# Spreading the differential heads' norm factors over the partitions: through DRAM instead of through TensorE

## The chip, the core and the metric

The kernel runs on one core of a Trainium2 chip. Such a core has five engines that each work through their own queue in order: TensorE (PE in the profile; its weight loads are PEld), VectorE (DVE), ScalarE (ACT), GpSimd (POOL) and SyncE (SP). SP and POOL issue the DMAs of this kernel; the transfers themselves run on 16 DMA engines. The metric is the device time of one execution in microseconds.

## The reference, cut to what matters

One decoder layer on 512 tokens of width 1024: two attention branches side by side, a gated merge, and a gated MLP. The branch that the change touches is differential attention with four heads. Each head has two softmax maps, takes their weighted difference, multiplies it with values of width 128, and then applies an RMS norm per head and token:

```python
def block_fn(args):
    qblk, n = args
    scores = jnp.einsum('bqhmd,bshmd->bhmqs', qblk, k).astype(jnp.float32) * scale
    ...
    p = jax.nn.softmax(scores, axis=-1)
    a = p[:, :, 0] - lam * p[:, :, 1]
    return jnp.einsum('bhqs,bshe->bqhe', a.astype(v.dtype), v)
...
out = out.reshape(b, s, DIFF_HEADS, DIFF_VDIM)
out = _rmsnorm(out, subln_g) * (1.0 - lam_init)
...
merged = (jax.nn.sigmoid(ga) * (out_a @ w_branch_swa[l])
          + jax.nn.sigmoid(gd) * (out_d @ w_branch_diff[l]))
```

So every head yields 512 norm factors, one for each token, and each of a head's 128 output channels of that token is multiplied by it.

## The kernel before, in words

All matrices are held as pairs of a rounded part (`hi`, made by a cast on ScalarE) and its remainder (`lo`, made by a subtraction on VectorE). A product is three matmuls: hi by hi, hi by lo, lo by hi (`mm3`, lines 121 to 124).

The differential stage lies at about 130 to 240 us of the span. Its outputs are kept transposed, with the 128 channels of a head on the partitions and the 512 tokens along the free dimension. The norm factors come out the other way round: `stats` (line 802) sums the squares with small matmuls into a tile of 128 partitions by 4 columns, token 128 n + p at partition p and column n, and VectorE and GpSimd turn these into the factors `rs` (the tile is `drs` in the profile). The factor has to be multiplied along the free dimension, alike on all partitions. So `turn_norm` (line 812) lets TensorE transpose each of the four columns, broadcast to 128 columns, into a PSUM bank `rb` of 128 by 512, which then holds the factors in every partition. VectorE multiplies the head's output `of` by it (line 816), ScalarE casts the product into `outd` hi, VectorE subtracts for `outd` lo (`split`, lines 117 to 119).

The order of TensorE's work is written out by hand. Beside the attention blocks run the projections of later steps: `fill(n)` (line 540) issues n steps of them, three matmuls of 512 columns each, and counts them. A piece of work can be hung on that count: `after(n, fn)` calls `fn` n steps later, `flush(kind)` calls what was put by under a kind. The loop over the 16 blocks s (head h = s // 4, block n = s % 4) fills 2 and then 4 steps a block, issues scores, softmax and transpositions (`td` in the profile, of the softmax results `sd`), and at n = 0 the values of the head before (`diff_values`). The sums of a head are flushed in the third block of the next head, its norm in the first block of the head after that, 12 steps later. The last head has no such blocks behind it: its sums come 10 steps (STAT_LAG) after its values, its norm 16 steps (NORM_LAG) after that.

The order on VectorE and ScalarE in this stage is not written out; the framework's scheduler chooses it from priorities and its own estimate, with some pieces pinned behind others (`tc.issue_after`). VectorE also prepares the weights (subtractions at line 119), adds up rows of the conditioning matrix (`arow`, lines 857 and 859, from tiles `ra` that SP loads), and evacuates score and transposition banks.

GpSimd's queue has little in this stage: per head one power for the norm (line 185), per finished conditioning row one small write to DRAM (`mod_rows`, line 882), and at its end the loads of `g1b` and its bias, which spread a conditioning row over all partitions (line 1067). The merge of the branches reads all four heads' `outd` from its first step on (`pB` in the profile).

Of the kernel before, what the change touches and what calls it, by code (L numbers as in the profile page):

```python
# [34 lines left out]
ADA_START = 4  # L35
V_LAG = 13
STAT_LAG = 10
NORM_LAG = 16
SWA_FILL = (2, 2, 5, 2, 2, 2, 2, 3)
DIFF_FILL = (3, 2, 4, 2)  # L40
WARM_FIRST = 3
# [13 lines left out]
def kernel(  # L55
# [44 lines left out]
    def tbank(name, shape=(P, S)):  # L100
        return bank("t", 2, list(shape), name)
# [15 lines left out]
    def split(hi, lo, src):  # L117
        cast = nc.scalar.copy(hi, src)
        return cast, nc.vector.tensor_sub(lo, src, hi.bitcast(F32))
# [368 lines left out]
    def evac(hi, lo, src, scale=None):  # L488
        if scale is None:
            nc.scalar.copy(hi, src)  # L490
            nc.vector.tensor_sub(lo, src, hi.bitcast(F32))
        else:
            nc.scalar.activation(hi, src, AF.Copy, scale=scale)
            return nc.vector.scalar_tensor_tensor(lo, src, scale, hi.bitcast(F32), ALU.mult, ALU.subtract)
# [66 lines left out]
            if tick[0] >= ADA_START and tick[0] % ADA_EVERY == 0:  # L561
                next(ada, None)

    beside = {"row": [], "sum": [], "norm": [], "turn": []}

    def after(n, fn):
        later.append([n, fn])
# [13 lines left out]
    hT = (hTh, hTl)  # L581


    class Pair:
        pass

    def swa_scores(i, blocks):
        if 0 in blocks:
            c = pairs[i] = Pair()
            c.mx, c.nm, c.lsum, c.es = (  # L590
                ap.tile([P, 2, NT], F32, tag=t, bufs=2, name=f"{t}{i}") for t in ("mx", "nm", "lsum", "es")
            )
            c.sb = [ap.tile([P, 2, P], F32, tag="st0", bufs=2, name=f"st{i}_0")]
            c.sb += [ap.tile([P, 2, 256], F32, tag="st", bufs=ST, name=f"st{i}_{n}") for n in range(1, NT)]
            c.pT = []
        c = pairs[i]
        sps = {
            (g, j): vbank(f"sw{i}_{g}_{j}").rearrange("p (a q) -> p a q", a=2)
            if len(blocks) == NT and (g, j) == (1, 1) else sbank(f"sw{i}_{g}_{j}", (P, 2, 256))
            for g in sorted({n // 2 for n in blocks}) for j in range(2)  # L600
        }
        for n in blocks:
            w = P if n == 0 else 2 * P
            k0 = max(0, n - 1) * P
            qs, ks = slice(n * P, (n + 1) * P), slice(k0, k0 + w)
            mm3_rows([
                (
                    sps[n // 2, j][:, n % 2, :w],
                    [qa[64 * j : 64 * j + 64, i, b, qs] for b in range(2)],
                    [ka[64 * j : 64 * j + 64, b, ks] for b in range(2)],  # L610
                )
                for j in range(2)
            ])
        for n in blocks:
            w = P if n == 0 else 2 * P
            if n == 2:
                c.first = c.last
            for j in range(2):
                with tc.high_priority(offset=HP):
                    c.last = nc.vector.tensor_tensor_reduce(  # L620
                        c.sb[n][:, j, :w], sps[n // 2, j][:, n % 2, :w], dsw[:, 256 - w : 256], 1.0, -3e38, ALU.add, ALU.max,
                        c.mx[:, j, n : n + 1],
                    )
# [151 lines left out]
    def diff_transpose(s):  # L775
        h, n = divmod(s, NT)
        if n == 0:
            aTs[h] = [ap.tile([P, 1664], F32R, tag=g, bufs=2, name=f"{g}{h}") for g in ("aTh", "aTl")]
        tp = tbank(f"td{h}_{n}")
        for k in range(n + 1):  # L780
            nc.tensor.transpose(tp[:, k * P : (k + 1) * P], probs[s][:, k * P : (k + 1) * P], ident)
        hi, lo = (a.rearrange("p (b q) -> p b q", q=P)[:, n : 4 * n + 1 : 3] for a in aTs[h])
        with tc.high_priority(offset=HP):
            evac(hi, lo, tp[:, : (n + 1) * P].rearrange("p (k q) -> p k q", q=P))

    def diff_values(h):
        t, (aTh, aTl) = heads[h], aTs[h]
        o = vbank(f"od{h}")
        for k in range(NT):
            q0 = k * P  # L790
            mm3(
                o[:, q0:], t[:, 4, k * P : (k + 1) * P], t[:, 5, k * P : (k + 1) * P],
                aTh[:, k * AW + q0 : k * AW + 512], aTl[:, k * AW + q0 : k * AW + 512],
                k == 0, k == NT - 1,
            )
        sq = ap.tile([P, S], F32, tag="tmp", bufs=2, name=f"sq{h}")
        of = ap.tile([P, S], F32, tag="of", bufs=2, name=f"of{h}")
        nc.scalar.activation(sq, o, AF.Square)
        nc.scalar.activation(of, o, AF.Copy, scale=sublnc)

        def stats():
            pss = tbank(f"pss{h}", (P, NT))
            for n in range(NT):
                nc.tensor.matmul(pss[:, n : n + 1], sq[:, n * P : (n + 1) * P], ones[:, 0:1], start=True, stop=True)
            rs, r0, r2 = (ap.tile([P, NT], F32, tag=t, bufs=2, name=f"{t}{h}") for t in ("drs", "dr0", "dr2"))
            nc.vector.reciprocal(r0, sums[h][:, 0])
            nc.vector.tensor_mul(r2, r0, r0)
            nc.vector.tensor_mul(r2, r2, pss)
            rstd_m2(rs, r2, NT, P, ap)
            nc.vector.tensor_mul(rs, rs, r0)  # L810

            def turn_norm():
                rb = tbank(f"rb{h}")
                for n in range(NT):
                    nc.tensor.transpose(rb[:, n * P : (n + 1) * P], rs[:, n : n + 1].to_broadcast([P, P]), ident)
                nc.vector.tensor_mul(of, of, rb)
                split(outd[0][:, h], outd[1][:, h], of)

            if h < 3:
                beside["norm"].append(turn_norm)  # L820
            else:
                after(NORM_LAG, turn_norm)

        if h < 3:
            beside["sum"].append(stats)
        else:
            after(STAT_LAG, stats)


    mod_rows = tc.dram_tile([4, D], F32, name="mod_rows")  # L830

    def ada_load(idx, hf, k):
        c0 = (2 + idx) * D + hf * S
# [55 lines left out]
    def add_gate_a(j):  # L889
        def gate(wts):  # L890
            o = fbank(f"pga{j}")
            yield from steps(o, wts, hT, KT)
            nc.scalar.activation(ta[:, j], o, AF.Tanh, scale=0.5)

        def load():
            if j % 2 == 0:
                r = raw_tile([P, 4, 2 * P], f"wba{j}")
                for a in range(2):
                    nc.sync.dma_start(
                        r[64 * a : 64 * a + 64],  # L900
                        wba[256 * a : 256 * a + 256, j * P : (j + 2) * P].rearrange("(i p) n -> p i n", p=64),
                    )

                with tc.issue_after(spread[-1].ins) if j == 0 else ExitStack():
                    pair_w["a"] = split_pair(r, [P, 4, 2 * P], f"wba{j}")
            return pair_w["a"]

        def branch(wts):
            o = fbank(f"pA{j}")
            rhs = [[outa[b][:, k] for k in range(4)] for b in range(2)]  # L910
            yield from steps(o, wts, rhs, 4, cl=slice(j % 2 * P, j % 2 * P + P))
            nc.vector.scalar_tensor_tensor(ta[:, j], ta[:, j], 1.0, o, ALU.add, ALU.mult)

        units.append((lambda: load_cols(win, COL_GA + j * P, f"wga{j}"), gate))
        units.append((load, branch))

    group_ahead, sums = [1], {}
    pairs, firsts, scored, probs, aTs = {}, {}, {}, {}, {}
    ada = ada_rows()
    add_head(0)  # L920
# [47 lines left out]
    for s in range(4 * DIFF_HEADS):  # L968
        h, n = divmod(s, NT)
        if s in (4, 8):  # L970
            add_head(h + 1)
        elif s == 12:
            add_gate_a(2)
            add_gate_a(3)
        ahead = s == 1
        fill(DIFF_FILL[1] - ahead)
        nxt = (s + 1, s + 2) if n % 2 and s < 15 else ()
        if nxt:
            flush("row")
            diff_scores(*nxt)  # L980
        if n == 1:
            diff_transpose(s)
        fill(DIFF_FILL[2] + ahead)
        if n == 2:
            flush("sum")
        elif n == 0:
            flush("norm")
        if n != 1:
            diff_transpose(s)
        if s == 13:  # L990
            group_ahead.clear()
        elif s > 13:
            flush("row")
        diff_softmax(*nxt)
        if n == 0 and h:
            diff_values(h - 1)
            fill(DIFF_FILL[3])
    for j in range(4, KT):
        add_gate_a(j)
    fill(4)  # L1000
    flush("norm")
    diff_values(DIFF_HEADS - 1)
    while units or loaded or current:
        fill(1)
# [936 lines left out]
```

## Time and profile before

| what | value |
|---|---|
| median of 3 runs | 692.78 us (692.33 to 694.1) |
| the profiled execution | 693.06 us, its span 691.3 us |
| granted TensorE clock | 0.996 |
| TensorE busy | 680.5 us, 98% of the span |
| VectorE busy | 565.3 us, 82% |
| ScalarE busy | 384.6 us, 56% |
| GpSimd busy | 82.1 us, 12% |
| transpositions of norm factors | 16 in 4 blocks, starting at 161.8 to 229.7 us |

In a row of a timeline the first number is the start in us from the span's start, the second the duration; then engine, line, operation, output tile <- input tiles, shapes, and in brackets how long the engine stood idle before and what ended that. In a row of stages stand the busy times of TensorE, its weight loads, VectorE, ScalarE and GpSimd, each with its count, then the granted clock, the DMA engines' busy share and GB/s. The matmuls' durations overlap: one starts before the one before it has ended.

### The profile page before, as it was taken

To read this page: it belongs to the slowest core of one execution; us is meant where nothing else is said; L and a number is where in the kernel's file an instruction comes from. 1 tells how busy PE (TensorE), PEld (TensorE's weight loads), DVE (VectorE), ACT (ScalarE), POOL (GpSimd) and SP (SyncE) were. 2 spreads that over 40 slices of the span, in tenths; PEclk is the share of its full clock that TensorE was granted. 3 is DMA by queue.
4 is the path that set the end of the run, shared out by engine and by line. 5 is a ranking of instruction groups with operands and counts; after the bars stand their busy time and mean duration, and the time that the engine had idled before them with its cause. 6 is when DMAs were issued, how large, how long until landed. Compare 5 with 4: busy or idle time off the path is not lost. (4 is left out here: it accounts for less than half of the span.)

```text
span 691.3 us, 11249 instructions
## 1 busy us (share of the span) xinstructions
PE 680.5 (98%) x4203; PEld 592.7 (86%) x4203; DVE 565.3 (82%) x1073; ACT 384.6 (56%) x686; POOL 82.1 (12%) x100
## 2 busy tenths in 40 slices
PE   8999999999999999999999999999999999999995
PEld 5787877788888888888889999999999999888884
DVE  5898987987885666663789988888888999979997
ACT  7676666545552323332477756655565666656665
POOL 3000000000001000000030101112111002540300
PEclk9999999999999999999999999999999999999998
DMA  9985454553455675229726798777978748997903
GB/s 307 328 258 165 140 156 151 154 163 96 138 138 169 212 217 180 91 95 315 230 56 129 166 214 197 167 173 215 206 215 217 155 149 207 196 195 199 167 1 121
DMA packets 115926, 121.81 MB, mean 176 GB/s; under 512 B 4447, under 2 KB 93344, under 8 KB 115872
## 3 DMA queue, kind: packets, MB, share of 16 engines
q1 hardware_dynamic: 96958, 95.09, 43.8%
q0 software_dynamic: 18720, 25.73, 22.2%
q8 instruction: 33, 0.54, 0.3%
q10 hardware_dynamic: 194, 0.28, 0.1%
q14 instruction: 21, 0.17, 0.1%
HBM read 118.97 MB, written 2.11 MB: 175 GB/s over the span
## 5 line engine op out<-in xcount | busy, mean ns | idle before, releaser
L1270 PE MATMUL up<-t,m_whi 128*128 128x256 f32 x512 | 93.1, 283 | 0.0
L1270 PEld LDWEIGHTS up<-t,m_whi 128*128 128x128 f32 x512 | 79.9, 192 | 0.0
L1270 PE MATMUL up<-t,m_wlo 128*128 128x256 f32 x256 | 72.4, 283 | 0.0
L1270 PE MATMUL up<-bh,p_whi 128*128 128x256 f32 x232 | 65.7, 283 | 0.0
L1270 PE MATMUL up<-bl,p_whi 128*128 128x256 f32 x232 | 65.7, 283 | 0.0
L1270 PE MATMUL up<-bh,p_wlo 128*128 128x256 f32 x232 | 65.7, 283 | 0.0
L859 DVE SCALAR_TENSOR_TENSOR arow<-ra,cs,arow 128x512 f32<-128x512 f32 x56 | 42.0, 749 | 20.0 <-DMA ra<-in_w_ada_dram 19.4
L1270 PEld LDWEIGHTS up<-t,m_wlo 128*128 128x128 f32 x256 | 49.2, 192 | 0.0
L1270 PEld LDWEIGHTS up<-bh,p_whi 128*128 128x128 f32 x232 | 44.5, 192 | 0.0
L1270 PEld LDWEIGHTS up<-bl,p_whi 128*128 128x128 f32 x232 | 44.5, 192 | 0.0
L1270 PEld LDWEIGHTS up<-bh,p_wlo 128*128 128x128 f32 x232 | 44.5, 192 | 0.0
L1179 POOL DMA_DIRECT2D s<-in_w_up_dram x21 | 27.0, 1361 | 140.8 <-DMA s<-in_w_up_dram 66.5
L1207 ACT CAST m_whi<-s 128x1024 fp32r<-128x1024 f32 x31 | 32.5, 1049 | 11.1 <-DVE s L1201 6.3
L1211 DVE TENSOR_TENSOR m_wlo<-s,m_whi 128x1024 fp32r<-128x1024 f32 x31 | 37.8, 1219 | 0.0
L1270 PE MATMUL up<-t,p_whi 128*128 128x256 f32 x176 | 32.2, 283 | 0.0
L882 POOL DMA_DIRECT2D mod_rows<-row x8 | 4.9, 614 | 204.9 <-ACT row L881 204.9
L1270 PEld LDWEIGHTS up<-t,p_whi 128*128 128x128 f32 x176 | 27.5, 192 | 0.0
L1277 ACT ACTIVATE gT<-a,cv 128x512 f32<-128x512 f32 x22 | 17.8, 816 | 16.9 <-DVE a L1312 15.8
L185 POOL TENSOR_TENSOR r<-ms,mhalf 128x1 f32<-128x1 f32 (+1 forms) x16 | 12.6, 791 | 120.9 <-DVE ms L183 73.1
L1207 ACT CAST p_whi<-wa 128x1024 fp32r<-128x1024 f32 x18 | 18.8, 1046 | 12.5 <-PE up L1270 12.5
L1211 DVE TENSOR_TENSOR p_wlo<-wa,p_whi 128x1024 fp32r<-128x1024 f32 x18 | 22.0, 1223 | 3.8 <-ACT p_whi L1207 3.8
L1270 PE MATMUL up<-t,p_wlo 128*128 128x256 f32 x88 | 24.9, 283 | 0.0
(491 smaller groups left out, 2064.9 us busy)
## 6 DMA issues: line engine op xcount, KB each, us to landing
ra<-in_w_ada_dram SPq DMA_DIRECT2D x32, 512.0 KB, 4.4
wa<-in_w_up_dram SPq DMA_DIRECT2D x22, 512.0 KB, 3.9
s<-in_w_up_dram SPq DMA_DIRECT2D x21, 512.0 KB, 4.5
s<-in_w_up_dram POOLq DMA_DIRECT2D x21, 512.0 KB, 6.6
adaw<-in_w_ada_dram SPq DMA_DIRECT2D x12, 512.0 KB, 7.6
w<-in_w_in_dram SPq DMA_DIRECT2D x12, 512.0 KB, 4.9
a<-in_w_up_dram SPq DMA_DIRECT2D x11, 512.0 KB, 4.5
b<-in_w_down_dram SPq DMA_DIRECT2D x10, 512.0 KB, 4.6
```

The lines of the kernel that those rows point to most:

```text
L185: nc.gpsimd.tensor_tensor(r0, ms, mhalf[:, :n], ALU.pow)
L859: nc.vector.scalar_tensor_tensor(ac, r[:, a], cc, ac, ALU.mult, ALU.add)
L882: nc.gpsimd.dma_start(mod_rows[idx, hf * S : (hf + 1) * S].rearrange("(g n) -> g n", g=4), row[0:P:32])
L1179: nc.gpsimd.dma_start(dst, upblock(*blk), accum_op=ALU.add)
L1207: nc.scalar.copy(W[J, name][0], R[J, SRC[name]])
L1211: nc.vector.tensor_sub(lo, R[J, SRC[name]], hi.bitcast(F32))
L1270: nc.tensor.matmul(o[u], w[:, k, cu], b[:, k], start=name in ("p1", "m5", "p2") and k == 0 and x == 0, stop=k == 3 and x == 2, skip_group_ ...
L1277: nc.scalar.activation(grow(j), av[J][:, u], AF.Identity, bias=cv[:, 66 + j : 67 + j], scale=cv[:, 44 + j : 45 + j])
```

## The change

The factors of a head go from SBUF to a row of 512 numbers in DRAM (`norm_rows`), with 4 bytes per run because they lie across the partitions, and from there a second DMA reads the row into all 128 partitions of `rb`, now an SBUF tile. Both are issued on GpSimd's queue, at the end of `stats`. The second waits for the first. `rb` takes the place of the tiles that held the first blocks of the sliding-window attention: these two are now one explicit tile `st0` with two halves, and `rb` has one buffer under the same tag. The product and its split (`scale_out`) are hung 24 steps behind the sums for all four heads, and pinned on VectorE behind the last evacuation recorded before them (`read`). The flush of the norms goes away; before the last head's values stand 6 steps instead of 4 and a flush. In the order of the changed program TensorE has four entries fewer (16 transpositions in blocks of four), GpSimd's queue eight DMAs more, and SP's queue is the same.

```diff
-NORM_LAG = 16
+NORM_LAG = 24
...
-            nc.vector.tensor_sub(lo, src, hi.bitcast(F32))
+            return nc.vector.tensor_sub(lo, src, hi.bitcast(F32))
...
+    st0 = ap.tile([P, 2, 2, P], F32, tag="st0", name="st0")
...
-            c.sb = [ap.tile([P, 2, P], F32, tag="st0", bufs=2, name=f"st{i}_0")]
+            c.sb = [st0[:, i % 2]]
...
-            evac(hi, lo, tp[:, : (n + 1) * P].rearrange("p (k q) -> p k q", q=P))
+            read.append(evac(hi, lo, tp[:, : (n + 1) * P].rearrange("p (k q) -> p k q", q=P)))
...
-            def turn_norm():
-                rb = tbank(f"rb{h}")
-                for n in range(NT):
-                    nc.tensor.transpose(rb[:, n * P : (n + 1) * P], rs[:, n : n + 1].to_broadcast([P, P]), ident)
-                nc.vector.tensor_mul(of, of, rb)
-                split(outd[0][:, h], outd[1][:, h], of)
-
-            if h < 3:
-                beside["norm"].append(turn_norm)
-            else:
-                after(NORM_LAG, turn_norm)
+            rb = ap.tile([P, S], F32, tag="st0", name=f"rb{h}")
+            nc.gpsimd.dma_start(norm_rows[h].rearrange("(n p) -> p n", p=P), rs)
+            nc.gpsimd.dma_start(rb, norm_rows[h].partition_broadcast(P))
+
+            def scale_out():
+                with tc.issue_after(read[-1].ins):
+                    nc.vector.tensor_mul(of, of, rb)
+                    split(outd[0][:, h], outd[1][:, h], of)
+
+            after(NORM_LAG, scale_out)
...
+    norm_rows = tc.dram_tile([DIFF_HEADS, S], F32, name="norm_rows")
...
-            nc.vector.scalar_tensor_tensor(ta[:, j], ta[:, j], 1.0, o, ALU.add, ALU.mult)
+            read.append(nc.vector.scalar_tensor_tensor(ta[:, j], ta[:, j], 1.0, o, ALU.add, ALU.mult))
...
-        elif n == 0:
-            flush("norm")
...
-    fill(4)
-    flush("norm")
+    fill(6)
     diff_values(DIFF_HEADS - 1)
```

More of the change, by code (lines that the diff above doesn't have):

```diff
@@ L562, in fill @@
                 next(ada, None)
-    beside = {"row": [], "sum": [], "norm": [], "turn": []}
+    beside = {"row": [], "sum": [], "turn": []}
     def after(n, fn):
@@ L911, in branch @@
             yield from steps(o, wts, rhs, 4, cl=slice(j % 2 * P, j % 2 * P + P))
-            nc.vector.scalar_tensor_tensor(ta[:, j], ta[:, j], 1.0, o, ALU.add, ALU.mult)
+            read.append(nc.vector.scalar_tensor_tensor(ta[:, j], ta[:, j], 1.0, o, ALU.add, ALU.mult))
         units.append((lambda: load_cols(win, COL_GA + j * P, f"wga{j}"), gate))
         units.append((load, branch))
-    group_ahead, sums = [1], {}
+    group_ahead, sums, read = [1], {}, []
     pairs, firsts, scored, probs, aTs = {}, {}, {}, {}, {}
```

## The prediction

> **What bounds the kernel now.** I read the page's first part, then who waited for whom on TensorE, then the busy times by stage, and only then single tiles. The first fence is the page's share of busy time, the longest of TensorE's waits inside the attention stages, and the busy time by stage.
>
> ```profile
> span 691.3 us, 11249 instructions
> PE 680.5 (98%) x4203; PEld 592.7 (86%) x4203; DVE 565.3 (82%) x1073; ACT 384.6 (56%) x686; POOL 82.1 (12%) x100
> ...
> PE tp L656 <- DVE st L644: 0.5, 1, 0.5
> ...
> 130.00:240.00 110.00, 110.00 (x612) 89.34 (x611) 83.12 (x209) 50.46 (x109) 8.79 (x13) 1.00 0.53 157
> 240.00:580.00 340.00, 339.88 (x2396) 318.72 (x2395) 275.81 (x390) 181.58 (x271) 36.95 (x35) 1.00 0.68 179
> 580.00:684.00 104.00, 103.87 (x473) 86.32 (x471) 97.44 (x147) 63.98 (x97) 28.58 (x26) 1.00 0.74 149
> ```
>
> From 130 us to 684 us TensorE (first busy column) is never without a matmul for more than 0.25 us in all, at full granted clock (the 1.00). So every microsecond of TensorE issue taken out of the differential stage (130 to 240) should move all that follows, and every wait put in front of TensorE should push it back. VectorE has 83 of 110 us busy there, so it has room, but it works in order: a wait on it can reach TensorE.
>
> **Part 1, the transpositions go.** Rows of the transposed factors, and the matmuls around two of the four blocks (start, duration):
>
> ```profile
> L815 PE MATMUL rb<-ident,drs x16: 271/272/273, 161.8 to 229.8; 128*128 128x128 f32 x16
> L816 DVE TENSOR_TENSOR of<-of,rb x4: 687/689/689, 162.5 to 230.1; 128x512 f32<-128x512 f32 x4
> L119 DVE TENSOR_TENSOR outdB<-of,outdA x4: 685/690/693, 163.8 to 233.0; 128x512 fp32r<-128x512 f32 x4
> ...
> 161.82 0.60 PE L815 MATMUL rb<-ident,drs 128*128 128x128 f32 x4
> 162.26 0.27 PE L781 MATMUL td<-ident,sd 128*128 128x128 f32 x1
> ...
> 229.23 0.39 PE L124 MATMUL pga<-hThA,wga_l 128*128 128x512 f32 x1
> 229.46 0.60 PE L815 MATMUL rb<-ident,drs 128*128 128x128 f32 x4
> 229.81 0.48 PE L122 MATMUL pga<-hThB,wga_h 128*128 128x512 f32 x1
> 230.13 0.39 PE L123 MATMUL pga<-hTlB,wga_h 128*128 128x512 f32 x1
> ```
>
> A transposition lasts 272 ns, but matmuls overlap, so starts count. A matmul of 512 columns is followed after 0.23 us (229.23, 229.46). Around the last block, 229.23 to 230.13 is 0.90 us for two such matmuls, which by themselves take 0.45: the block costs 0.45. The first block holds its follower back from 161.82 to 162.26: 0.44. Taken for four heads: 4 x 0.445 = 1.8 us. Bounds: 0.35 per block (229.46 to 229.81), 1.4 us; and all sixteen durations, 16 x 0.272 = 4.4 us. I take 1.8, since starts are what TensorE's queue passes on. The Trainium skill, "TensorE: Matmul & The Clock Gate", Part 4: PE-mode transpose, puts a transposition inside a kernel at about 275 ns; by that the gain would be 16 x 0.275 = 4.4 us. The row's 272 ns agrees with it, the spacing of starts does not.
>
> VectorE's product reads the factors from SBUF instead of PSUM. Its row is 689 ns, and the subtraction beside it, all from SBUF, 690: zero.
>
> **Part 2, two DMAs per head on POOL's queue.** No row shows a DMA of 4-byte runs. Nearest rows: POOL's issue of 512 runs (L1179), the small write to DRAM (landing least, median, most), and POOL's broadcast reads.
>
> ```profile
> L1179 POOL DMA_DIRECT2D s<-in_w_up_dram x21 | 27.0, 1361 | 140.8 <-DMA s<-in_w_up_dram 66.5
> ...
> DMA to landing us min/median/max: 1.6/3.1/4.2
> ...
> s_t<-in_w_up_dram POOLq DMA_DIRECT2D x1, 512.0 KB, 11.3
> g1b<-mod_rows POOLq DMA_DIRECT2D x1, 512.0 KB, 4.8
> xn<-in_b_ada_dram POOLq DMA_DIRECT2D x1, 512.0 KB, 5.7
> g2b<-mod_rows POOLq DMA_DIRECT2D x2, 256.0 KB, 6.2
> ```
>
> The write also has 512 runs (128 partitions x 4): 1.4 us to issue, 3.1 to land. The read is g2b's twin, 256 KB out of a 2 KB row: 6.2. Chain: 10.7 us. Bounds: 1.6 + 4.8 = 6.4, and 1.4 + 4.2 + 11.3 = 16.9. I take 10.7, by the twin.
>
> How long may it be? VectorE meets the wait where the changed program has the product. That order shows it behind the reciprocal that ran at 174.09 (head 0), and behind the `ta` products at 196.85, 218.80 and 236.53 (heads 1 to 3). The rows: factors ready (drs), that predecessor, the next softmax product (sd), and TensorE's transposition (td) that needs it.
>
> ```profile
> 156.47 0.16 DVE L810 TENSOR_TENSOR drs<-drs,dr 128x4 f32<-128x4 f32 x1
> 174.09 0.16 DVE L767 RECIPROCAL dls<-dls 128x1 f32<-128x1 f32 x1
> 175.91 0.61 DVE L769 SCALAR_TENSOR_TENSOR sd<-sd,dls,sd 128x384 f32<-128x384 f32 x1
> 177.24 0.53 PE L781 MATMUL td<-ident,sd 128*128 128x128 f32 x3
> 181.60 0.16 DVE L810 TENSOR_TENSOR drs<-drs,dr 128x4 f32<-128x4 f32 x1
> 194.50 0.68 DVE L744 CUSTOM_DVE_ANT_0 sd<-sd,ddf 128x512 f32<-128x512 f32 x1
> 196.19 0.74 DVE L859 SCALAR_TENSOR_TENSOR arow<-ra,cs,arow 128x512 f32<-128x512 f32 x1
> 196.85 0.68 DVE L912 SCALAR_TENSOR_TENSOR ta<-ta,pA 128x512 f32<-128x512 f32 x1
> 196.96 0.37 SPq L835 DMA_DIRECT2D ra<-in_w_ada_dram  x1
> 198.10 0.62 DVE L769 SCALAR_TENSOR_TENSOR sd<-sd,dls,sd 128x384 f32<-128x384 f32 x1
> 200.77 1.54 DVE L859 SCALAR_TENSOR_TENSOR arow<-ra,cs,arow 128x512 f32<-128x512 f32 x2 [0.50 <-DMA ra<-in_w_ada_dram]
> 201.49 0.53 PE L781 MATMUL td<-ident,sd 128*128 128x128 f32 x3
> 205.84 0.16 DVE L810 TENSOR_TENSOR drs<-drs,dr 128x4 f32<-128x4 f32 x1
> 216.19 0.62 POOL L882 DMA_DIRECT2D mod_rows<-row  x1 [12.48 <-ACT row L881]
> 218.80 0.68 DVE L912 SCALAR_TENSOR_TENSOR ta<-ta,pA 128x512 f32<-128x512 f32 x1
> 221.85 0.16 DVE L810 TENSOR_TENSOR drs<-drs,dr 128x4 f32<-128x4 f32 x1
> 236.53 0.68 DVE L912 SCALAR_TENSOR_TENSOR ta<-ta,pA 128x512 f32<-128x512 f32 x1
> 237.13 1.22 DVE L1075 TENSOR_TENSOR g1b<-g1b,xn 128x1024 f32<-128x1024 f32 x1
> 253.63 0.39 PE L122 MATMUL pB<-outdA,wbd 128*128 128x512 f32 x1
> ```
>
> Windows from factors ready to predecessor's end: 174.25 - 156.63 = 17.6; 197.53 - 181.76 = 15.8; 219.48 - 206.0 = 13.5; 237.2 - 222.0 = 15.2 us. All exceed 10.7, so I cost the chain at nothing; its cover is 24 steps of projection matmuls. If that cover fails, the price is rival C.
>
> Queued behind the two on POOL: the next `mod_rows` write (closest behind head 2: 216.19, 10.2 us after its factors, while the chain holds POOL for 4.5 and 0.6) and then the next head's power; nothing lost. After head 3 the loads of `g1b` and its bias stand behind the read, which waits for the write: 222.0 + 4.5 for the write, 0.6 for each of two issues, then 5.7 to land the bias: near 233.4. VectorE adds them at 237.13: hidden by 3.7 us. SP's queue keeps its order.
>
> One buffer now serves all four `rb`, so head h's read waits for head h-1's product. The program puts each product before the next head's factors: nothing.
>
> **Part 3, the product moves later.** From 12 steps after the sums (head 2: 10, head 3: 16) to 24; head 3's values come two steps later, because two steps replace the last flush. TensorE does the same steps, in another order: zero. The consumer is the merge at 253.63; head 3's product near 237.9, its cast and subtraction (0.69) end by 240: 13 us to spare.
>
> On VectorE the product now stands in denser work. Head 0: sd's 384-wide product ended at 176.52 and TensorE wanted it at 177.24; the changed order has one `arow` step fewer ahead of it and the product (0.69 for 0.75), while TensorE comes 0.44 earlier: about 0.3 us spare. Head 1: product and one `arow` step stand ahead of sd, and that step waits for `ra`, which landed at 200.77, 3.8 after its issue at 196.96, itself released by the `arow` step at 196.19. In the changed order the releasing step stands ahead of the score reduction at 194.50: done near 194.9, landing near 198.7, then `arow` (0.75) and sd (0.62) by 200.0, TensorE there at 201.49 - 0.9 = 200.6: 0.6 us spare. So zero, but thin.
>
> **The sum.** Transpositions -1.8, all else 0. The profiled execution is 693.06 us (span 691.3, 1.8 around it): 691.3. The median of the runs, 692.78, is 0.3 lower: 691.0.
>
> **The rivals.** **B, a thin spare gives way.** If head 1's `ra` lands 1 to 2 us later, or head 0's sd slips, TensorE waits 0.2 to 1.4 us and the gain is part gone: 691.2 to 692.8, say 692.0. For it: VectorE waited for `ra` at 200.77 already. Against: that load's issue moves forward too.
>
> **C, slower: the DMA chain outgrows its window.** VectorE stops in front of the softmax products, TensorE in front of td. A chain of c us costs c - 17.6 - 0.3 at head 0 and c - 15.8 - 0.6 at head 1 (heads 2 and 3 have no transposition close behind). Gain gone at c = 18.1, slower by 0.3% from c = 19.1, 20 us gives 2.1 + 3.6: 696.7. For it: no row shows 4-byte runs. Against: the upper bound, 16.9, costs only 0.5. The Trainium skill, "SBUF — State Buffer", SBUF: two separate sides, warns that a DMA issued from GpSimd starves while VectorE runs an operation in a two-port mode, and gives 3.1 us for one that takes 0.62 alone. By an estimate from that page two DMAs would add 5 us: a chain of 15.7 and still about 691. No row here shows such a pair.
>
> **D, faster: the whole durations go.** If a block holds TensorE for 4 x 0.272, the gain is 4.4: 688.4. For it the row; against it the starts.
>
> **How the numbers follow.** A (forecast, 690.5 to 691.6) 0.56; B 0.15; C 0.17; D 0.12. A measurement tells 0.3%, 2.1 us, from no change: the bounds are 690.7 and 694.9. A's 1.8 us lies just inside; four tenths of A falls beyond 690.7 with the scatter of the runs (692.33 to 694.1). Faster 0.22 + 0.12 = 0.34; same 0.34 + 0.15 = 0.49; slower 0.17. Range 689.6 to 694.8 leaves out half of D and three quarters of C, 0.19.
>
> **What would show it.** Right: no TensorE gap over 0.3 us between 150 and 240, td of head 1 about 0.9 us earlier, the merge at about 251.9; VectorE's waits for `rb` near zero. Wrong: VectorE waiting for `rb`'s DMA or for `ra` directly before a td, or DMAs of `norm_rows` landing after more than 9 us.

## The result: slower by 4.6%

The changed kernel takes 724.5 us (median of 4 runs, 721.29 to 728.66) against 692.56 us before: a ratio of 1.0463, 95% interval 1.0399 to 1.0527, or some 32 us. The forecast was 691.0 us with a range up to 694.8. The profiled execution of the changed kernel is 728.66 us with a span of 726.8, the longest of its four; against the profiled execution before (span 691.3) it is 35.5 us longer, and the traces below explain that difference.

First the page of the changed kernel: busy times, and the row of VectorE's `arow` steps (busy time, mean ns; idle time before them and what ended it).

```profile
span 726.8 us, 11228 instructions
PE 689.2 (95%) x4187; PEld 598.3 (82%) x4187; DVE 564.3 (78%) x1073; ACT 382.9 (53%) x686; POOL 87.4 (12%) x108
L861 DVE SCALAR_TENSOR_TENSOR arow<-ra,cs,arow 128x512 f32<-128x512 f32 x56 | 41.9, 748 | 58.5 <-DMA ra<-in_w_ada_dram 57.9
```

TensorE's longest waits (total, times, longest, us):

```profile
PE pA L122 <- DVE ta L914: 14.6, 2, 8.3
PE td L783 <- DVE dls L769: 5.1, 1, 5.1
PE td L783 <- DVE sd L771: 2.9, 1, 2.9
PE pss L806 <- DVE qkv L491: 2.0, 1, 2.0
```

VectorE's longest wait, and the same wait in the kernel before:

```profile
DVE arow L861 <- DMA ra<-in_w_ada_dram: 57.9, 14, 14.9
...
DVE arow L859 <- DMA ra<-in_w_ada_dram: 19.4, 15, 2.9
```

The busy time by stage, in the columns of the kernel before:

```profile
130.00:240.00 110.00, 97.18 (x516) 78.32 (x514) 66.28 (x183) 43.33 (x100) 9.59 (x13) 0.92 0.50 113
240.00:580.00 340.00, 326.56 (x2187) 300.41 (x2188) 259.14 (x368) 164.84 (x247) 40.32 (x41) 0.97 0.70 179
```

TensorE, which was busy in all 110 us of the first stretch before, now stands still for 12.8 of them, and the granted clock there is 0.92 instead of 1.00. VectorE did not get more work (564.3 us, 565.3 before): it waited 57.9 us for `ra`, where the kernel before waited 19.4. The stage and its way to the merge are where the difference lies. From the first sums of a head (`pss`) to the first matmul of the gates behind the stage (`pgd`) the kernel before takes 90.6 us (152.2 to 242.8) and the changed one 124.0 (151.9 to 275.9). From there to the merge (`pB`) it is 10.8 and 13.0. What lies before and behind differs by 0.3 us at most.

Of these 35.6 us, TensorE's waits between the first sums and the merge make up 26.3. The rest goes to a lower clock: the trace's clock record shows half the full clock for four stretches of 6.8 to 10.2 us, each during or right behind one of the longer waits, and a matmul of 512 columns then takes 0.63 us in place of 0.39:

```profile
205.51 0.39 PE L124 MATMUL pga<-hThB,wga_l 128*128 128x512 f32 x1
...
216.32 0.63 PE L124 MATMUL pA<-outah,wba_l 128*128 128x512 f32 x1
```

By an estimate from these numbers the lower clock costs some 9 to 11 us: 35.6 less 26.3 is 9.3, and 1.8 more if the transpositions took what the prediction says.

GpSimd's timeline tells what came first: the write of each head, and the read that follows.

```profile
156.65 0.84 POOL L815 DMA_DIRECT2D norm_rows<-drs  x1 [1.08 <-DVE dmx L746]
168.52 0.59 POOL L816 DMA_DIRECT2D rb<-norm_rows  x1 [11.03 <-PE sd L129]
186.26 0.82 POOL L815 DMA_DIRECT2D norm_rows<-drs  x1 [1.10 <-DVE drs L812]
197.04 0.56 POOL L816 DMA_DIRECT2D rb<-norm_rows  x1 [9.95 <-DMA norm_rows<-drs]
220.76 0.82 POOL L815 DMA_DIRECT2D norm_rows<-drs  x1 [2.59 <-DVE drs L812]
233.69 0.56 POOL L816 DMA_DIRECT2D rb<-norm_rows  x1 [12.10 <-DMA norm_rows<-drs]
250.59 0.82 POOL L815 DMA_DIRECT2D norm_rows<-drs  x1 [1.09 <-DVE drs L812]
261.83 0.56 POOL L816 DMA_DIRECT2D rb<-norm_rows  x1 [10.41 <-issue]
```

Rows of the view of DMAs (KB each, median us from issue to landing):

```profile
norm_rows<-drs POOLq DMA_DIRECT2D x4, 2.0 KB, 11.0
rb<-norm_rows POOLq DMA_DIRECT2D x4, 256.0 KB, 5.7
```

The landings of the loads of `ra`, in the changed kernel and in the kernel before:

```profile
DMA to landing us min/median/max: 3.8/4.8/15.4
...
DMA to landing us min/median/max: 3.8/4.4/5.2
```

A write of 2 KB lands after 11.0 us (median), twice as long as the read of 256 KB behind it. And a load of `ra` (512 KB), whose longest landing before was 5.2 us, now takes up to 15.4. VectorE's timeline shows these late loads behind the writes of all four heads, with the long waits at heads 1 to 3:

```profile
171.87 0.49 DVE L859 TENSOR_SCALAR arow<-ra,cs 128x512 f32<-128x512 f32 x1 [4.02 <-DMA ra<-in_w_ada_dram]
201.20 1.54 DVE L861 SCALAR_TENSOR_TENSOR arow<-ra,cs,arow 128x512 f32<-128x512 f32 x2 [8.78 <-DMA ra<-in_w_ada_dram]
237.70 1.54 DVE L861 SCALAR_TENSOR_TENSOR arow<-ra,cs,arow 128x512 f32<-128x512 f32 x2 [14.89 <-DMA ra<-in_w_ada_dram]
244.72 0.68 DVE L914 SCALAR_TENSOR_TENSOR ta<-ta,pA 128x512 f32<-128x512 f32 x1
245.32 0.68 DVE L820 TENSOR_TENSOR of<-of,rb 128x512 f32<-128x512 f32 x1
267.28 1.54 DVE L861 SCALAR_TENSOR_TENSOR arow<-ra,cs,arow 128x512 f32<-128x512 f32 x2 [14.01 <-DMA ra<-in_w_ada_dram]
```

And TensorE's timeline shows what it then waits for:

```profile
214.80 0.87 PE L783 MATMUL td<-ident,sd 128*128 128x128 f32 x3 [5.06 <-DVE dls L769]
245.46 0.80 PE L122 MATMUL pA<-outah,wba_h 128*128 128x512 f32 x1 [8.27 <-DVE ta L914]
270.61 0.79 PE L122 MATMUL pA<-outah,wba_h 128*128 128x512 f32 x1 [6.33 <-DVE ta L914]
```

The last three of the waits shown, 8.78 + 14.89 + 14.01 = 37.7 us, are two thirds of the 57.9; each ends 4.0 to 5.5 us after the read that waits for the write was issued (197.04, 233.69, 261.83). VectorE works in order, so the `ta` products and softmax pieces behind the waiting `arow` step come late, and TensorE stops for them. The product with `rb` (245.32) has no wait of its own in brackets: the row had landed by then. So the loss is not where a reader of the diff would look, in front of `rb`, but in front of another load.

### The profile page after: what moved, and what is told of

Its sections match the earlier page's. It is cut to its first block, busy times and chain, and to the rows that moved or that the text cites. A ratio compares the mean times of both kernels' runs of the same rounds, so it can differ in the third digit from the quotient of the medians.

```text
span 726.8 us, 11228 instructions
## 1 busy us (share of the span) xinstructions
PE 689.2 (95%) x4187; PEld 598.3 (82%) x4187; DVE 564.3 (78%) x1073; ACT 382.9 (53%) x686; POOL 87.4 (12%) x108
## 4 chain that ended last, share of the span: by engine, by line
PE 80%; DMA 12%; DVE 5%; ACT 1%; issue 1%; POOL 0%; SPq 0%; DVEq 0%; ACTq 0%; POOLq 0%
PE up L1269 31%; PE dc L1884 14%; DMA ra<-in_w_ada_dram 10%; PE a L385 3%; PE oc L1325 2%; PE oc L1329 2%; PE oc L1326 2%; PE pgd L122 2%; PE pgd L123 2%; PE pgd L124 2%; DVE arow L861 1%; DMA w<-in_w_in_dram 1%; PE pw L122 1%; PE pB L122 1%; PE pB L123 1%
## 5 line engine op out<-in xcount | busy, mean ns | idle before, releaser
L861 DVE SCALAR_TENSOR_TENSOR arow<-ra,cs,arow 128x512 f32<-128x512 f32 x56 | 41.9, 748 | 58.5 <-DMA ra<-in_w_ada_dram 57.9
L766 ACT ACTIVATE sd<-sd,dmx 128x128 f32<-128x128 f32 (+3 forms) x32 | 17.6, 553 | 26.0 <-DVE dmx L756 26.0
L122 PE MATMUL pA<-outah,wba_h 128*128 128x512 f32 x32 | 15.8, 493 | 14.6 <-DVE ta L914 14.6
```

Source lines behind the costliest of these rows:

```text
L122: nc.tensor.matmul(o, lh, rh, start=start, stop=False)
L766: exp = nc.scalar.activation(pm[m], pm[m], AF.Exp, bias=mx[:, m : m + 1], scale=slope, accum_out=ls)
L861: nc.vector.scalar_tensor_tensor(ac, r[:, a], cc, ac, ALU.mult, ALU.add)
```

## The experiments

A theory to start with: the write of 4-byte runs holds the DMA engines, and all that is loaded meanwhile comes late. Its rivals: the read of 256 KB beside the loads; the new order of VectorE's work; and GpSimd's way of issuing.

**The write alone, the read alone, the order alone, and the write in long runs.**

```diff
 write alone (kernel before, behind the factors)
+            nc.gpsimd.dma_start(norm_rows[h].rearrange("(n p) -> p n", p=P), rs)
 read alone (kernel before; rx in the tile st0)
+            nc.gpsimd.dma_start(rx, final_g[0:S].partition_broadcast(P))
 order alone (changed kernel, no DMAs)
             def scale_out():
+                rb = tbank(f"rb{h}")
+                for n in range(NT):
+                    nc.tensor.transpose(rb[:, n * P : (n + 1) * P], rs[:, n : n + 1].to_broadcast([P, P]), ident)
 rows of 512 bytes (changed kernel, hung 6 steps behind the sums)
 ...
+                nc.tensor.transpose(pn, rs, ident)
 ...
+                    nc.scalar.copy(rows4, pn)
+                nc.gpsimd.dma_start(norm_rows[h].rearrange("(n p) -> n p", p=P), rows4)
+                nc.gpsimd.dma_start(rb, norm_rows[h].partition_broadcast(P))
```

> The kernel before, with only the write added: each head's factors go to DRAM in 512 runs of 4 bytes, nobody reads them, the transpositions stay. Theory W (the write of 4-byte runs holds up the DMA engines, so the weight and conditioning loads come late): 15 to 35 us slower than before, VectorE's waits for ra near 55 us, landing of the write near 11 us. Theory O (the new order on VectorE and the late product): no change, within 2 us. Theory R (the broadcast read): no change, within 2 us.

> The kernel before, with only a broadcast read of 256 KB per head added on GpSimd's queue (a row of an input into all partitions, into the tile that rb has in the changed kernel; nobody uses it), the transpositions stay. Theory W: within 2 us of before. Theory R: 15 to 35 us slower. Theory O: within 2 us.

> The changed kernel without its DMAs: the product 24 steps behind the sums and pinned as there, the last head's values 2 steps later, but the factors spread by TensorE's transpositions just ahead of the product. Theory W: within 2 us of before, no TensorE wait above 1 us in the stage. Theory O: 15 to 35 us slower, VectorE waiting for ra ahead of the softmax products.

> The changed kernel, but one small TensorE transposition turns the 128 by 4 factors into 4 rows of 128, ScalarE copies them to SBUF, and the write goes to DRAM in 4 runs of 512 bytes; read, lag and product as in the changed kernel. Theory W: 690.5 to 693, the write lands in 2 to 4 us, no TensorE wait above 1 us in the stage. Theories O and R: as slow as the changed kernel, 715 to 728.

| kernel | median, us | ratio to before (95%) | write lands, median us | longest `ra`, us |
|---|---|---|---|---|
| write alone | 713.07 | 1.0294 (1.0261 to 1.0328) | 9.9 | 11.4 |
| read alone | 693.19 | 1.0013 (1.0001 to 1.0024) | none | 5.3 |
| order alone | 697.4 | 1.0062 (1.0044 to 1.008) | none | 5.1 |
| rows of 512 bytes | 694.18 | 1.002 (1.0009 to 1.0031) | 2.3 | 5.0 |

The write, which nobody reads and which stands in an otherwise unchanged kernel, costs 20 us. It gives the changed kernel's picture in small, though VectorE waits less for `ra` than the 55 us that were expected. Its longest wait there:

```profile
DVE arow L862 <- DMA ra<-in_w_ada_dram: 40.7, 16, 8.9
```

TensorE's:

```profile
PE td L781 <- DVE dr L806: 5.6, 1, 5.6
PE pA L122 <- DVE ta L915: 5.4, 2, 4.1
```

The landings of its write:

```profile
DMA to landing us min/median/max: 8.9/9.9/10.4
```

The order alone takes 4.3 us more, a figure that none of the theories had. It is not all the order's: of TensorE's 2.9 us of waiting in that stage, 2.1 are this run's own.

```profile
PE td L783 <- DVE of L819: 2.1, 2, 1.9
```

There the transpositions still put `rb` into a PSUM bank of the kind that `td` needs as well, and `td` waits until the product has read it. In the changed kernel `rb` lies in SBUF and this wait cannot come. A cleaner figure stands further down. The same numbers by the same route, but first turned by one TensorE transposition into 4 runs of 512 bytes, cost 1.4 us in place of 32 (expected were 693 us at most). The read alone says less than it was meant to: nothing made it wait, so its four issues ran ahead to 105.3 to 120.0 us, in front of the stage. What a read within the stage costs is told further down.

**What about the write is slow: the number of runs, their size, their distance, or the queue?**

```diff
 a quarter: 128 runs of 4 bytes, 4 bytes apart
+            nc.gpsimd.dma_start(norm_rows[h, 0:P].rearrange("(p n) -> p n", n=1), rs[:, 0:1])
 spread: 512 runs of 4 bytes, 512 bytes apart (16 for P: 64 bytes apart)
+    norm_rows = tc.dram_tile([DIFF_HEADS, NT, P, P], F32, name="norm_rows")
+            nc.gpsimd.dma_start(norm_rows[h, :, :, 0].rearrange("n p -> p n"), rs)
 other queue: as the write alone
+            nc.scalar.dma_start(norm_rows[h].rearrange("(n p) -> p n", p=P), rs)
 runs of 16 bytes (changed kernel)
-            nc.gpsimd.dma_start(norm_rows[h].rearrange("(n p) -> p n", p=P), rs)
+            nc.gpsimd.dma_start(norm_rows[h].rearrange("(p n) -> p n", n=NT), rs)
-                    nc.vector.tensor_mul(of, of, rb)
+                    o3 = of.rearrange("q (n p) -> q n p", p=P)
+                    nc.vector.tensor_mul(o3, o3, rb.rearrange("q (p n) -> q n p", n=NT))
```

> As the write alone, but each head writes only one of its four columns: 128 runs of 4 bytes to DRAM instead of 512; nobody reads them. Write alone with 512 runs cost 20.3 us and landed in 9.9 us. If every run costs time (theory W by runs): landing near 3 to 4 us, 0 to 5 us slower than before. If one such write holds things up whatever its size: landing near 10 us, 15 to 20 us slower.

> As the write alone with all 512 runs of 4 bytes, but every run goes to a DRAM address of its own, 512 bytes from the next, so that no two runs of different DMA engines meet in one piece of memory. If the runs hurt because they are small or many: landing near 10 us and 15 to 20 us slower than before, as the write alone. If they hurt because neighbours in DRAM are written by different engines at once: landing in 2 to 5 us, within 3 us of before.

> As the write alone, 512 runs of 4 bytes to the same DRAM row, but issued on ScalarE's queue instead of GpSimd's. If the DRAM side holds up the DMA engines: landing near 10 us, 15 to 25 us slower than before. If GpSimd's way of issuing does: landing in 2 to 4 us, within 3 us of before (and a wait of ScalarE for the factors).

> The kernel before with a write beside it of 512 runs of 4 bytes that lie 64 bytes apart, read by nobody. With 4 bytes apart the time rose by 20 us, with 512 bytes apart by nothing. If what collides is a stretch of DRAM of some 64 bytes or fewer, it stays at 692 to 694 us with landings of 2 to 4 us. If the stretch is larger (512 runs at 64 bytes take 32 KB, against 256 KB), landings lie between 3 and 9 us and the time rises by some part of the 20 us.

> The changed kernel, but each row of norm factors lies in DRAM as the tile has it: partition p writes its 4 numbers next to each other, 128 runs of 16 bytes instead of 512 of 4, and scale_out reads the broadcast row in that order (every fourth number). No transposition is left on TensorE. Theory 1 (only runs as small as 4 bytes collide when they lie next to each other): the write lands within about 4 us as the spread one did (2.3 to 4.3 us), the wait of arow for ra falls from 57.9 us to about 27 us, the time is about 694 us. Theory 2 (neighbouring small runs collide whatever their count, also at 16 bytes): the write lands in 8 to 9 us as with 128 runs of 4 bytes, and the time is 712 to 725 us.

| write, per head | in | median, us | ratio to before (95%) | lands, us | longest `ra`, us |
|---|---|---|---|---|---|
| 512 runs of 4 bytes, adjacent | before | 713.07 | 1.0294 (1.0261 to 1.0328) | 9.9 | 11.4 |
| 128 runs of 4 bytes, adjacent | before | 711.16 | 1.0268 (1.025 to 1.0287) | 8.7 | 13.2 |
| 512 runs of 4 bytes, adjacent, ScalarE's queue | before | 712.83 | 1.0293 (1.0274 to 1.0311) | 9.7 | 12.8 |
| 512 runs of 4 bytes, 64 bytes apart | before | 692.75 | 1.0 (0.9989 to 1.0011) | 2.6 | 5.8 |
| 512 runs of 4 bytes, 512 bytes apart | before | 692.9 | 1.0007 (0.9993 to 1.0022) | 2.7 | 6.7 |
| 128 runs of 16 bytes, adjacent | changed | 696.11 | 1.0051 (1.0036 to 1.0067) | 2.4 | 5.8 |

So it is not the number: a quarter of the runs costs nearly as much. It is not the size by itself: 4 bytes are harmless as soon as the next run lies 64 bytes away. It is not the issuing queue: on ScalarE's, which otherwise issues four DMAs of this kernel, the write is as slow. It is 4-byte runs that lie next to each other in DRAM; with 16-byte runs, equally adjacent, nine tenths of the loss are gone (696.11 us leave 3.4 of the 32; about 694 us had been expected). Distances between 4 and 64 bytes were not run. And in each harmful write the neighbours come from different partitions, so whether 4-byte runs of one partition would do the same harm stays open. The landings of the quarter, the shortest of the harmful writes:

```profile
DMA to landing us min/median/max: 8.1/8.7/9.1
```

And those of the 512 runs that lie 64 bytes apart:

```profile
DMA to landing us min/median/max: 2.3/2.6/4.3
```

Why neighbours hurt each other, no run shows. The packet records in the traces only narrow it. In the changed kernel the write's own packets, 16 of 128 bytes, start within 0.2 to 0.4 us of each other, 1.5 to 2.0 us after the issue; the landing is signalled 8 to 10 us behind the last of them. In that time single 2 KB packets of other loads take up to 5.5 us; their median is 84 ns, and in the same stretch of the kernel before (150 to 290 us) none takes more than 1.3 us. The Trainium skill, "DMA: Bandwidth & Descriptors", Specifications, says that the DMA engines do a read-modify-write below 512 bytes. Size alone does not explain these runs: 4 bytes at a distance of 64, and 16 bytes side by side, are both far below it and land in 2.4 to 2.6 us.

**Where the rest comes from.** The write alone costs 20 us, the order alone 4, the change 32. The two kernels here multiply by another row in place of the factors, so their output is not the layer's, and they tell the time alone.

```diff
 order and spread (changed kernel; 512 bytes apart, another row read)
-            nc.gpsimd.dma_start(norm_rows[h].rearrange("(n p) -> p n", p=P), rs)
-            nc.gpsimd.dma_start(rb, norm_rows[h].partition_broadcast(P))
+            nc.gpsimd.dma_start(norm_rows[h, :, :, 0].rearrange("n p -> p n"), rs)
+            nc.gpsimd.dma_start(rb, final_g[0:S].partition_broadcast(P))
 write unread (changed kernel)
-            nc.gpsimd.dma_start(rb, norm_rows[h].partition_broadcast(P))
+            nc.gpsimd.dma_start(rb, final_g[0:S].partition_broadcast(P))
```

> The changed kernel, but the 512 numbers of a head are written 512 bytes apart, and the row that is read back and multiplied is another one, of 2 KB, that lies in DRAM already: so the product has the wrong factors, and the work and the transfers are those of the change without the collision. If the new order of VectorE alone costs 4 us as in the run with the order alone, and no DMA adds to it: 695 to 698 us, with transpositions gone perhaps 693 to 696. If the two DMAs cost something of their own that the runs on the old order could not show, because there nobody waited for them: above 700 us.

> The changed kernel with its 4-byte write, but the read that follows fetches another row of 2 KB, which does not wait for the write (the product then has the wrong factors). Theory 1 (the rest of the loss is that late ra loads and weights meet the new order of VectorE, and nobody waits for rb): 720 to 727 us, as the change. Theory 2 (the rest is the chain of write, read and product, the read of 256 KB being started only when the slow write has landed): 708 to 716 us, as the write alone.

With the new order, no transpositions, a harmless write and reads of which three of four fall into the stage (174.1 to 220.5 us), the time is 694.93 us (1.0044, 1.0026 to 1.0063): 3 us for all of that. With the 4-byte write and a read that does not wait for it, it is 720.58 us (1.0399, 1.0382 to 1.0416), 28 us above the kernel before. So the 20 us of the write and the 3 of the order become 28 together. The 5 us by which the whole exceeds its parts fit late loads that meet an order with `arow` steps ahead of what TensorE needs (VectorE waits 53.9 us for `ra` there, 40.7 with the write alone); this is argued from the waits, no run separates it. The 4 us left to the changed kernel belong to the read's waiting for the write, or to scatter: the intervals of the two ratios overlap, and VectorE never waited for `rb` in the changed kernel. That part stays open.

**A version without the loss.** Three kernels look for one.

```diff
 rows tuned (rows of 512 bytes)
-NORM_LAG = 24
+NORM_LAG = 28
-            after(6, write)
+            after(10, write)
 old order (kernel before: DMAs in 16-byte runs, product hung as turn_norm was, NORM_LAG 24, fill(6))
-                rb = tbank(f"rb{h}")
-                for n in range(NT):
-                    nc.tensor.transpose(rb[:, n * P : (n + 1) * P], rs[:, n : n + 1].to_broadcast([P, P]), ident)
 later product (runs of 16 bytes)
-NORM_LAG = 24
+NORM_LAG = 28
```

> The version with 4 runs of 512 bytes, its transposition 10 steps behind the sums instead of 6 (there TensorE waited 2.3 us for the factors) and the product 28 steps behind instead of 24. Theory W: no TensorE wait above 0.5 us in the differential stage, that stage 1 to 2 us shorter than in the kernel before, 690.8 to 692.0. If the new order on VectorE itself costs, 693 or more.

> The order of VectorE's work of the kernel before, and the norm rows by two DMAs in runs of 16 bytes, without transpositions of norm factors on TensorE; the product of heads 0 to 2 stands where it stood before, that of head 3 eight steps later than before. If only the new order is left to pay in the run with 16-byte runs (696.1 us, 3.4 us above before): 691 to 693 us, the 16 transpositions' issue time (1.8 us) being the gain. If the write and the read do not land in the two steps of a head between the sums and the product: VectorE waits for rb directly before the product, and the time is 693 to 698 us.

> The kernel with 16-byte runs and the new order, with the product 28 steps after the sums in place of 24. If the 3.4 us of that kernel over the kernel before come from where the product and its split fall in VectorE's order: 692 to 694.5 us, with td waiting for dls less than 3.4 us in all. If they come from arow's steps standing ahead of the softmax, which the lag does not move: 695.5 to 697 us.

Rows tuned: 693.53 us (1.0013, 1.0001 to 1.0025). Later product: 699.98 us (1.0097, 1.0079 to 1.0115), worse than 24 steps, against both expectations; TensorE's wait of `td` for `dls` shrank from 3.4 to 2.9 us, and other small waits grew. Old order: 709.31 us (1.0235, 1.0217 to 1.0254), above both expectations (698 us at most), and here, for the first time, VectorE does wait for `rb`. Its two longest waits in that kernel:

```profile
DVE of L820 <- DMA rb<-norm_rows: 18.2, 4, 5.6
DVE arow L864 <- DMA ra<-in_w_ada_dram: 12.7, 12, 2.0
```

Two of the four places in its timeline, each with the step at which the factors were ready:

```profile
155.08 0.16 DVE L812 TENSOR_TENSOR drs<-drs,dr 128x4 f32<-128x4 f32 x1
162.33 1.07 DVE L820 TENSOR_TENSOR of<-of,rb 128x512 f32<-128x512 f32 x1 [3.52 <-DMA rb<-norm_rows]
...
212.68 0.16 DVE L812 TENSOR_TENSOR drs<-drs,dr 128x4 f32<-128x4 f32 x1
221.18 1.07 DVE L820 TENSOR_TENSOR of<-of,rb 128x512 f32<-128x512 f32 x1 [5.08 <-DMA rb<-norm_rows]
```

Even with harmless runs the chain from factors to landed row takes 162.33 - 155.24 = 7.1 us and 221.18 - 212.84 = 8.3 us. In the kernel before, the product of head 0 starts 5.9 us behind its factors (162.5 - 156.63), and the old order leaves little more than that. The 24 steps of the change are there to hide this chain, and they do: with the later product and harmless runs VectorE waits nowhere for `rb`. Their price is not one figure: the versions that have the later product and harmless runs stand 1.0 to 7.4 us above the kernel before. No version ran faster than it.

## Why the prediction was wrong

- **Part 1, the transpositions (1.8 us of issue time).** Not seen singly. The new order with harmless DMAs and no transpositions has the ratio 1.0044, the new order with transpositions 1.0062: 0.0018 apart, or 1.2 us. The intervals overlap, and the second kernel has the wait for `rb`'s bank on top, so this neither proves the 1.8 nor speaks against it.
- **Part 2, the price of the write: the step that failed.** It was taken as 1.4 us to issue, from the nearest row of 512 runs, and 3.1 to land, from the `mod_rows` write, which has 4 runs of 512 bytes. The issue took 0.82 us, the landing 11.0. The text said that no row showed 4-byte runs and then drew the bounds from rows of long runs all the same.
- **Part 2, the reach of the write: the larger half of the same failure.** Even the right landing, put into that sum, gives little: with 11.0 for the write and 5.7 for the read, a chain of 16.7 us, rival C's formula yields 0.3 us at head 1. The cost was laid on those who wait for `rb`; it fell on the loads that were under way beside the write, and on those who wait for them. That a load would come late was weighed only as rival B's 1 to 2 us at one head, and not as an effect of the write.
- **Part 2, "all exceed 10.7": held by luck.** From factors ready to row landed, by the trace's landing times, the four heads took 18.4, 16.0, 18.5 and 17.8 us, more than the windows of 17.6, 15.8, 13.5 and 15.2 that were worked out. The product still found its row landed, because the late loads had put it back as well: it starts 20 to 26 us behind its factors.
- **"Every wait put in front of TensorE should push it back":** true and too little. The waits of 26.3 us brought some 9 to 11 more by the lower clock (the estimate above).
- **Rival C, slower:** right in its sign and in its doubt (4-byte runs), wrong in its place. VectorE never waited for `rb` in the changed kernel. The mechanism is real where the window is short: with the old order the time is 16.7 us longer (709.31 against 692.57) and VectorE waits 18.2 us for `rb`. That heads 2 and 3 have no transposition close behind is true and not enough: TensorE's longest waits, 8.27 and 6.33 us, stand there, in front of `pA`, for the `ta` products that the prediction read only as what stands ahead of the product with `rb`.
- **Rival B, a late `ra` at head 1:** the right place, wait and load, at 1 to 2 us instead of 8.78, and then at heads 2 and 3 too.
- **Part 3, the new order (put at zero):** too low. With harmless DMAs it is 3 us above the kernel before, although the transpositions are gone. The spare that the prediction called thin held in that run: between 150 and 240 us TensorE waits 0.2 us at most in front of a `td`. It waits 2.4 us in front of `pgd` instead, for `ta`.
- **The doubt drawn from the Trainium skill**, "SBUF — State Buffer", SBUF: two separate sides, that a DMA issued from GpSimd starves beside a two-port operation of VectorE: no run here shows it. On ScalarE's queue the write lands in 9.7 us, on GpSimd's in 9.9.
- **What would show it wrong** was named rightly: VectorE waiting for `ra`, and `norm_rows` landing after more than 9 us.

## What to carry to other kernels

A DMA whose kind no row of the trace shows has no upper bound from rows of other kinds: measure it alone, beside the old kernel, before anything is built on it. Ask not only who waits for a transfer but which transfers are in flight beside it, and which engine takes them in order. When a small tile must go to DRAM across its partitions, let each partition write its neighbours together (16 bytes were enough here), or turn it first.

## What the runs showed of the hardware

- Writes of 4-byte runs side by side in DRAM land after 8.7 to 11.0 us (medians of the runs), whether they are 128 or 512 and whichever of the two queues issues them, and meanwhile a 512 KB load on another queue took up to 15.4 us (5.2 before). At a distance of 64 bytes the same 512 runs land in 2.6 us.
- During or right behind TensorE's longer waits its granted clock fell as well, to 0.83 from 180 to 200 us, where TensorE is busy throughout behind a wait of 2.9 us, and to 0.74 from 200 to 220 us, so that a wait cost more than its own length. Behind the wait of 1.65 us at 281.70 it did not fall:

```profile
180.00:200.00 20.00, 20.00 (x104) 15.76 (x103) 9.53 (x34) 8.62 (x21) 3.00 (x4) 0.83 0.42 92
200.00:220.00 20.00, 12.94 (x54) 10.63 (x54) 14.13 (x36) 5.69 (x13) 1.03 (x1) 0.74 0.43 119
220.00:240.00 20.00, 17.18 (x89) 13.77 (x88) 5.04 (x9) 3.98 (x7) 1.96 (x3) 1.00 0.53 67
```

- VectorE's product took 1.07 us where it read every fourth number of `rb`, against 0.68 us in a row. The Trainium skill, "SBUF — State Buffer", Door 1: The DMA port swizzle, says that SBUF has lines of 16 bytes and that every access in a new line costs extra; a step of four 4-byte numbers is such a line. The two rows agree with that; no run tried another step.
